# A hybrid decoder block on one core: first weight casts on VectorE, two early input tiles, norm 2's first product in token halves, residual products ahead at the end

## The chip, the cores and the metric

One NeuronCore of one Trainium2 chip runs the whole block in one launch. The metric is the device time of that core in microseconds, as the median of several runs; lower is better.

## The reference

One layer, T = 512 tokens of D = 1024 channels, all float32. The convolution branch has 1024 channels, the recurrence 1280, the channel mixer 2816.

```python
h = rmsnorm(x, norm1_g)
z = h @ w_in + b_in                      # 1024 -> 6656
z_glu, z_rx, z_rg, z_ga, z_gb = split(z) # 2048, 1280, 1280, 1024, 1024
u = z_glu[:, :1024] * sigmoid(z_glu[:, 1024:])
u = silu(layernorm(causal_depthwise_conv(u, 31 taps)))
y_a = u @ conv_w_out + conv_b_out
hb = rg_lru(causal_depthwise_conv(z_rx, 4 taps), wa, ba, wx, bx, lambda)
y_b = (hb * gelu(z_rg)) @ lru_w_out
x = x + (sigmoid(z_ga) * y_a + sigmoid(z_gb) * y_b) @ w_mix_out
h = rmsnorm(x, norm2_g)
x = x + (silu(h @ ffn_w1) * (h @ ffn_w3)) @ ffn_w2
return rmsnorm(x, norm_f_g)
```

## The kernel before

**Number format.** Every float32 operand of a matmul is split into a high part in float32r and a low part, the difference (`split_to`, L121: a cast by `copy`, ScalarE's unless told otherwise, then a subtraction on GpSimd or VectorE). One product of the reference is three on TensorE: high by high, high by low, low by high (`mm3`, L514). With `lo_last`, all products that need only the high weights come first.

**Weights.** They arrive in chunks of 128 x 1024 (`emit_chunk`, L145): a load by SyncE's queue into one of four buffers (`raws`, names raw_...), the cast on ScalarE, the difference on GpSimd (for w_in) or VectorE (later weights), into one of five split buffers (`hls`, names hl_...). `weights(key, ahead)` (L178) emits chunks up to four beyond the one wanted. Only chunks of w1 and w3 for norm 2 and what follows it are made from two loads; some of them are sums of four quarters that VectorE adds (L351) or a DMA accumulates (L349).

**Order.** A scheduler orders each engine's instructions by their dependences and by the order of the program. Inside `tc.manual_schedule(engines=...)` the listed engines keep the order in which the code is written; `tc.issue_after` puts work behind a named instruction. PSUM has six banks under `bank` and two under `bank2`.

**Start (L493 to L618).** TensorE first multiplies a tile of ones by itself (WARM times, one multiply is two records in the profile). The input comes in four row blocks of 128 tokens. `norm1_rows` (L575) takes a block's sum of squares and scales it in place (L579). Parameter vectors are loaded as rows (`load_rows`, L469) and transposed by TensorE (`rows_turned`, L503): norm1_g and b_in are the first group, since `turn_half` (L556) needs norm1_g. `turn_half` transposes 128 x 128 blocks of one half of the tokens (256), scales them by the norm's parameter on ScalarE (the high part, h, L566) and takes the low part on VectorE (L567). While the second half of the tokens is not there yet, the first EARLY_IN output tiles of w_in are computed on the first half alone (`early_mm`, L586): EARLY = 2 makes four tiles (0, 8, 1, 9), two of them started ahead of the second turn and two behind it; then all four are finished on the second half. The other tiles take all 512 columns in one matmul. PE, ScalarE, VectorE and SyncE are in written order here.

**Middle.** `ORDER` (L227) lists the tiles of w_in and the steps of the recurrence; the 31-tap convolution runs on VectorE beside it (`beside`, L670). `Quartered` and `Sevenfold` (L250, L896) form the products with w_mix_out and ffn_w2 from seven block products in place of eight.

**Norm 2 (L1006 to L1136).** `mix_end` ends the first residual sum, takes the norm's sums and transposes the first half of the tokens, in written order on PE, ScalarE and VectorE; its last lines emit one weight chunk and scale row blocks 2 and 3. The channel mixer's 22 output tiles of w1 and w3 go in pairs k and k + 11. Pairs 1 and 2 (FIRST) begin with two block products on the first token half (`f_product`, L1054, PSUM names fr1, fr2), which cover the wait for blocks 2 and 3. Then the second half is turned (L1076), with ScalarE's h and VectorE's low parts as at the start; VectorE also forms the plain sum of high and low, h2f (`full`, L1071), first for token half LO, and for HI within `f_inputs` (L1083), which makes the operands of the seven products from it. Pair 0 (PLAIN) is computed as plain products, first f1_0 and f3_0, then tiles 11. `ended` and `f_out` (L1111, L1115) finish the products of FIRST with a silu on ScalarE; then come the first products of pairs 3 and 4 (NEXT), and the others (PSUM names fa, fb, fe, ft).

**End (L1170 to L1225).** `out_end` adds up the second residual sum in four row blocks, two halves each. Blocks 0 and 1 are ready while TensorE still works (`finish(0)`, `finish(1)`); for blocks 2 and 3 the second half is ready early, the first half is in PSUM (r1) and gets its last products from `third` (hold = 3 of them kept back). `finish` (L1181) squares both halves with a sum on ScalarE, takes the reciprocal root, multiplies each half by the root and norm_f_g, and stores both. With `rest` (blocks 2 and 3), the product of the second half with norm_f_g is taken ahead of `third` and scaled by ScalarE behind it:

```python
begun = rstd_begin(x2[t][1], jk[0])
if rest:
    vec.tensor_tensor(out=o[1], in0=x2[t][1], in1=gf[1], op=ALU.mult)
    rest()
r = rstd_end(begun, first, jk[1])
```

Of the kernel before, what the change touches and what calls it, by code (L numbers as in the profile page):

```python
# [13 lines left out]
P = 128  # L14
# [11 lines left out]
NT = T // P  # L26
# [10 lines left out]
WARM = 12  # L37
# [49 lines left out]
def tile_block(ctx, tc, a, out):  # L87
# [33 lines left out]
    def split_to(h, l, full, eng, copy=act.copy):  # L121
# [9 lines left out]
        return h, l  # L131

    def split(name, full, eng, p_=None, copy=act.copy):
        p_ = p_ or pairt(name)
        return split_to(*p_, full, eng, copy)
# [9 lines left out]
    def emit_chunk():  # L145
# [16 lines left out]
        if where != "long":  # L162
            hl = hls.tile([P, 2, 1024], F32R, tag="hl", name=f"hl_{key}")
            h, l = split_to(hl[:, 0, :n], hl[:, 1, :n], rv, lo)
# [9 lines left out]
    def emit_to(n):  # L174
        while emitted[0] < min(len(chunks), n):
            emit_chunk()
# [278 lines left out]
    row_at = lambda c: (0, c) if c < n_first else (1 + (c - n_first) // P, (c - n_first) % P)  # L455
# [44 lines left out]
    for i in first:  # L500
        load_rows(i)
# [54 lines left out]
    def turn_half(name, rows, gname, dest, hf, bk, some=range(ND)):  # L556

        cs = slice(hf * 256, hf * 256 + 256)
        for c in some:
# [5 lines left out]
            h, l = (v[:, cs] for v in dest[c])  # L565
            act.activation(h, ps[:, :256], AF.Copy, scale=g)  # L566
# [15 lines left out]
    EARLY = 2  # L582
# [12 lines left out]
    with tc.manual_schedule(engines={ET.PE, ET.Activation, ET.DVE, ET.SP}):  # L595
        norm1_rows(0)
        norm1_rows(1)
        rows_turned(0, n_first)
        emit_to(1)
        turn_half("tx", xt, "norm1_g", h1p, 0, [bank, bank, bank, bank2])  # L600
        emit_to(2)
        load_x(2)
        load_x(3)
        norm1_rows(2)
        norm1_rows(3)
        emit_to(3)
# [7 lines left out]
        early_mm(2, 0)  # L614
        early_mm(3, 0)
        rows_turned(n_first, n_rows)
        for i in range(4):
            early_mm(i, 1)  # L618
# [457 lines left out]
    turned = turn_half("th", xs, "norm2_g", h2p, 1, [bank2])  # L1076
    h2 = parts_of(h2p)
    with tc.issue_after(turned):
        emit_to(emitted[0] + 3)
# [3 lines left out]
    def f_inputs(ks):  # L1083
        for k in ks:
            a1, a2 = h2f[k], h2f[k + 4]
            full(k, HI)
            full(k + 4, HI)
# [23 lines left out]
    def ended(k, c11, r2):  # L1111
        add(c11, r2, c11)
        f_out(c11, o7.uv[k][0][:, LO])
# [8 lines left out]
    for i, j in enumerate((PLAIN, PLAIN + KF)):  # L1122
        p1, p3 = bank(f"f1_{j}"), bank(f"f3_{j}")
        mm3(p1, w_tiles(f"f1_{j}", ND), h2)
        mm3(p3, w_tiles(f"f3_{j}", ND), h2)
# [55 lines left out]
    def finish(t, ps=None, rest=None):  # L1181
# [3 lines left out]
        first = x2[t][0] if ps is None else ps  # L1185
        begun = rstd_begin(x2[t][1], jk[0])
        if rest:
            vec.tensor_tensor(out=o[1], in0=x2[t][1], in1=gf[1], op=ALU.mult)
            rest()
        r = rstd_end(begun, first, jk[1])  # L1190
        vec.scalar_tensor_tensor(out=o[0], in0=first, scalar=r, in1=gf[0], op0=ALU.mult, op1=ALU.mult)
        if rest:
            act.activation(o[1], o[1], AF.Copy, scale=r)
        else:
            vec.scalar_tensor_tensor(out=o[1], in0=x2[t][1], scalar=r, in1=gf[1], op0=ALU.mult, op1=ALU.mult)
# [3 lines left out]
    def out_end(second, plus, r1, r2, r7, third):  # L1199
# [18 lines left out]
        finish(0)  # L1218
        for k in range(kh - hold, kh):
            outq.get(k, "t4")  # L1220
        finish(1)
        for i in range(2):
            finish(2 + i, r1[i], lambda: third(i, range(kh - hold, kh)))
# [35 lines left out]
```

## Time and profile before

| | |
|---|---|
| device time, median of 3 runs | 800.8 us (800.53 to 800.96) |
| profiled execution: its own time | 800.93 us |
| profiled execution: span | 799.2 us, mean granted TensorE clock 0.998 |
| TensorE matmul (PE) | 788.9 us, 99% of the span |
| TensorE weight load (PEld) | 689.5 us, 86% |
| VectorE (DVE) | 675.5 us, 85% |
| ScalarE (ACT) | 472.1 us, 59% |
| GpSimd (POOL) | 231.6 us, 29% |
| DMA | 140.29 MB, mean 176 GB/s |

In rows of the profile, PE is the matmul side of TensorE, PEld its weight load, DVE VectorE, ACT ScalarE, POOL GpSimd, and SPq SyncE's queue. A row of the order of time has the start in us from the start of the span, the time taken in us, the engine, the line of the kernel (L123), the operation, what it writes <- what it reads, shapes, and a count where equal neighbours are joined; in square brackets stands what the engine waited for and how long. A row of groups has the count, then least, median and greatest duration in ns, then the time from the first to the last. In the waits, "PE tx L563 <- DVE x L579: 0.9, 2, 0.6" reads: TensorE's instructions of L563 that write tx waited for VectorE's L579 0.9 us in total, two times, 0.6 at the longest. The time of one matmul record covers a pipelined operation, so its pace is read from start to start.

### The profile page before, as it was taken

How to read it: one execution, taken by the hardware profiler on the slowest of the kernel's cores; microseconds unless marked ns; L12 is line 12 of the kernel's file. 1: busy time of each engine (PE TensorE's matmuls, PEld its weight loads, DVE VectorE, ACT ScalarE, POOL GpSimd, SP SyncE). 2: the span in 40 equal slices, each digit the busy share in tenths (PEclk: the TensorE clock that was granted, in tenths of full speed). 3: DMA queues.
4: the chain of work that ended last, by engine and by line, in shares of the span. 5: the costliest groups of instructions: out<-in, count | busy, mean ns of one | idle time of the engine just before them, and what ended most of it. 6: DMA issues, size and time to landing. Idle time of an engine off the chain costs nothing.

```text
span 799.2 us, 12191 instructions
## 1 busy us (share of the span) xinstructions
PE 788.9 (99%) x4374; PEld 689.5 (86%) x4374; DVE 675.5 (85%) x1027; ACT 472.1 (59%) x678; POOL 231.6 (29%) x182
## 2 busy tenths in 40 slices
PE   8999999999999999999999999999999999999997
PEld 7988888888888888888888888999999999888885
DVE  4699899999989988796787889978778887889756
ACT  7546595898668855563335574545455555577443
POOL 3565867687766855130000000000000000000000
PEclk9999999999999999999999999999999999999999
DMA  7945647378564754468947536477555553676552
GB/s 212 239 122 165 174 150 212 121 213 237 164 193 144 225 177 125 128 193 266 282 153 246 172 107 183 120 178 190 147 132 133 133 132 106 205 265 203 198 172 105
DMA packets 184624, 140.29 MB, mean 176 GB/s; under 512 B 14279, under 2 KB 162163, under 8 KB 184563
## 3 DMA queue, kind: packets, MB, share of 16 engines
q1 hardware_dynamic: 183123, 134.27, 55.4%
q0 software_dynamic: 1440, 5.24, 3.5%
q8 instruction: 34, 0.56, 0.3%
q14 instruction: 27, 0.22, 0.1%
HBM read 113.79 MB, written 18.64 MB: 166 GB/s over the span
## 4 chain that ended last, share of the span: by engine, by line
PE 91%; DVE 4%; DMA 2%; ACT 2%; issue 1%; SPq 0%; DVEq 0%; POOLq 0%; ACTq 0%
PE z L523 35%; PE or L933 13%; PE ft L1060 7%; PE yb L523 7%; PE fa L1060 6%; PE ya L523 5%; PE mxr L933 5%; PE fe L1060 3%; PE g L807 3%; PE fr L1060 3%; PE fb L1060 2%; PE f L523 1%; DMA raw_fb<-in_ffn_w_dram 1%; DMA raw_fb<-raw_fb 1%; DMA x<-in_x_dram 1%
## 5 line engine op out<-in xcount | busy, mean ns | idle before, releaser
L682 DVE SCALAR_TENSOR_TENSOR cv<-u,par,cv 128x511 f32<-128x511 f32 (+16 forms) x240 | 162.0, 728 | 2.3 <-ACT cv L679 2.2
L119 POOL TENSOR_TENSOR hl_in<-raw_in,hl_in 128x1024 fp32r<-128x1024 f32 x52 | 125.9, 2426 | 82.8 <-ACT hl_in L123 80.4
L349 POOL DMA_DIRECT2D raw_fb<-raw_fb x10 | 8.7, 874 | 299.3 <-DVE raw_fb L351 186.6
L119 POOL TENSOR_TENSOR ows<-ows 128x256 f32<-128x256 f32 x66 | 57.2, 870 | 37.5 <-DMA ows<-in_ffn_w_dram 34.5
L123 ACT CAST hl_in<-raw_in 128x1024 fp32r<-128x1024 f32 x52 | 54.2, 1043 | 10.2 <-PE z L523 6.5
L123 ACT CAST hl_ft<-raw_fb 128x1024 fp32r<-128x1024 f32 x40 | 41.8, 1048 | 28.9 <-DVE raw_fb L351 12.7
L119 DVE TENSOR_TENSOR hl_ft<-raw_fb,hl_ft 128x1024 fp32r<-128x1024 f32 x40 | 48.6, 1219 | 9.7 <-ACT hl_ft L123 9.6
L119 DVE TENSOR_TENSOR hl_fb<-raw_fb,hl_fb 128x1024 fp32r<-128x1024 f32 x30 | 36.6, 1220 | 9.2 <-ACT hl_fb L123 8.9
L523 PE MATMUL z<-h10h,hl_in 128*128 128x512 f32 (+1 forms) x112 | 42.2, 378 | 1.0 <-DVE h10l L567 1.0
L523 PE MATMUL z<-h13h,hl_in 128*128 128x512 f32 (+1 forms) x112 | 41.7, 374 | 0.0
L523 PE MATMUL z<-h14h,hl_in 128*128 128x512 f32 (+1 forms) x112 | 41.7, 374 | 0.0
L523 PE MATMUL z<-h15h,hl_in 128*128 128x512 f32 (+1 forms) x112 | 41.7, 374 | 0.0
L523 PE MATMUL z<-h11h,hl_in 128*128 128x512 f32 (+1 forms) x112 | 41.7, 374 | 0.0
L523 PE MATMUL z<-h16h,hl_in 128*128 128x512 f32 (+1 forms) x112 | 41.7, 374 | 0.0
L523 PE MATMUL z<-h17h,hl_in 128*128 128x512 f32 (+1 forms) x112 | 41.7, 374 | 0.0
L523 PE MATMUL z<-h12h,hl_in 128*128 128x512 f32 (+1 forms) x112 | 41.7, 374 | 0.0
L351 DVE TENSOR_TENSOR raw_fb<-raw_fb,raw_fb 128x1024 f32<-128x1024 f32 x20 | 24.5, 1225 | 16.9 <-DMA raw_fb<-in_ffn_w_dram 16.6
L119 DVE TENSOR_TENSOR hl_ob<-raw_ob,hl_ob 128x1024 fp32r<-128x1024 f32 (+1 forms) x23 | 27.0, 1172 | 10.5 <-ACT hl_ob L123 7.6
L123 ACT CAST hl_ob<-raw_ob 128x1024 fp32r<-128x1024 f32 (+1 forms) x23 | 23.4, 1016 | 20.7 <-PE or L933 14.7
L123 ACT CAST hl_fb<-raw_fb 128x1024 fp32r<-128x1024 f32 x30 | 31.4, 1047 | 6.7 <-PE mxr L933 3.7
L1060 PE MATMUL fe<-hs_0h,hl_ft 128*128 128x256 f32 x160 | 30.8, 284 | 0.4 <-DVE hl_ft L119 0.4
L1060 PE MATMUL ft<-hs_1h,hl_ft 128*128 128x256 f32 x160 | 30.4, 283 | 0.0
(965 smaller groups left out, 2610.1 us busy)
## 6 DMA issues: line engine op xcount, KB each, us to landing
raw_in<-in_w_in_dram SPq DMA_DIRECT2D x52, 512.0 KB
raw_fb<-in_ffn_w_dram SPq DMA_DIRECT2D x96, 256.0 KB
ows<-in_ffn_w_dram SPq DMA_DIRECT2D x44, 256.0 KB
os<-ows SPq DMA_DIRECT2D x22, 512.0 KB
raw_ob<-in_ffn_w_dram SPq DMA_DIRECT2D x33, 256.0 KB
raw_ot<-os SPq DMA_DIRECT2D x33, 256.0 KB
raw_lo<-in_lru_w_out_dram SPq DMA_DIRECT2D x16, 320.0 KB
raw_fb<-raw_fb POOLq DMA_DIRECT2D x10, 512.0 KB, 4.5
```

Of the source, the lines that this page charges most:

```text
L119: return eng.tensor_tensor(out=o, in0=x, in1=y, op=ALU.subtract)
L123: copy(h, full)
L349: pool_e.dma_start(out=q, in_=y, accum_op=ALU.add)
L351: vec.tensor_tensor(out=q, in0=q, in1=y, op=ALU.add)
L523: pe.matmul(ps, l, r, start=i == 0, stop=i == n - 1)
L682: vec.scalar_tensor_tensor(out=acc[c][:, s:], in0=u[c][:, : T - s], scalar=dw(c, s), in1=acc[c][:, s:], op0=ALU.mult, op1=ALU.add)
L807: pe.matmul(ps, l, r, start=k == 0, stop=k == len(mms) - 1)
L933: pe.matmul(banks[i], l_[:, ts], r_, start=start and n == 0, stop=stop and n == 2, skip_group_check=again)
L1060: pe.matmul(ps[:, HALVES[i]], lw[:, 4 * i + c, :], rx_, start=not (again or i or c or m), stop=bool(i and c == 3 and m == 2), skip_group_c ...
```

## The change

- WARM goes from 12 to 21.
- The casts of the first two weight chunks are done by VectorE (`vec.tensor_copy`), no longer by ScalarE. The third chunk is emitted behind the loads of all parameter rows, with the fourth.
- EARLY goes from 2 to 1: two tiles of w_in (0 and 8) are worked in token halves. Both start on the first half ahead of the second turn; both are finished behind it. The transposes of b_in's rows move behind the second turn, into a tile of their own; b_in's rows are loaded behind x's blocks 2 and 3.
- Norm 2: TensorE's order from the second turn on is written by hand. f1_0 is computed in token halves in four steps, each of four transposes (two channel blocks of the second half) and twelve matmuls of 256 columns. For this half, ScalarE writes h2f itself from the transposes (`full` given), casts the high part from it, and VectorE takes the difference; `f_inputs` no longer adds up h2f for HI. f3_0 takes the low weights last. The silu of FIRST comes behind the last h2f.
- End: `finish` is split. The squares and products of the second halves of blocks 2 and 3 are written ahead of both `third`. Blocks 0 to 2 get their second half by that product and a scaling on VectorE; only block 3 is scaled by ScalarE.

```diff
@@ -34,7 +34,7 @@
 RAW = 4
 HL = 5
 AHEAD = 4
-WARM = 12
+WARM = 21
 
 FEW, MANY = 32, 112
 
@@ -128,11 +128,11 @@
             last = sub(eng, l, full, h.bitcast(F32))
         if eng is pool_e:
             newest["sub"] = last.ins
-        return h, l
+        return h, l, last
 
     def split(name, full, eng, p_=None, copy=act.copy):
         p_ = p_ or pairt(name)
-        return split_to(*p_, full, eng, copy)
+        return split_to(*p_, full, eng, copy)[:2]
 
 
     chunks = []
@@ -142,7 +142,7 @@
     def wchunk(key, src, kt, cols, where="hl", lo=pool_e, after=None):
         chunks.append((key, src, kt, cols, where, lo, after))
 
-    def emit_chunk():
+    def emit_chunk(copy=act.copy):
         if emitted[0] == GATES_AT:
             load_gates()
         key, src, kt, cols, where, lo, after = chunks[emitted[0]]
@@ -161,7 +161,7 @@
             newest["load"] = nc.sync.dma_start(rv.rearrange("p (k n) -> p k n", k=kt), src).ins
         if where != "long":
             hl = hls.tile([P, 2, 1024], F32R, tag="hl", name=f"hl_{key}")
-            h, l = split_to(hl[:, 0, :n], hl[:, 1, :n], rv, lo)
+            h, l, _ = split_to(hl[:, 0, :n], hl[:, 1, :n], rv, lo, copy)
             if after:
                 after(rv, h)
             held[key] = (h.rearrange("p (k n) -> p k n", k=kt), l.rearrange("p (k n) -> p k n", k=kt))
@@ -171,9 +171,9 @@
                 for i in range(2)
             ]
 
-    def emit_to(n):
+    def emit_to(n, copy=act.copy):
         while emitted[0] < min(len(chunks), n):
-            emit_chunk()
+            emit_chunk(copy)
 
     def weights(key, ahead=AHEAD):
         i = next(i for i, c in enumerate(chunks) if c[0] == key)
@@ -452,7 +452,12 @@
     n_rows = sum(n for _, n in ROWS)
     n_first = ROWS[0][1] + ROWS[1][1]
     par = consts.tile([P, n_rows], F32, name="par")
-    row_at = lambda c: (0, c) if c < n_first else (1 + (c - n_first) // P, (c - n_first) % P)
+    starts = (0, ROWS[0][1], n_first)
+
+    def row_at(c):
+        b = sum(c >= s_ for s_ in starts) - 1
+        return b + (c - starts[b]) // P, (c - starts[b]) % P
+
     at, col, parts = 0, {}, []
     for name, n in ROWS:
         col[name] = at
@@ -497,8 +502,7 @@
     first = [i for i, (lo, _, _) in enumerate(parts) if lo < n_first]
     load_x(0)
     load_x(1)
-    for i in first:
-        load_rows(i)
+    load_rows(first[0])
 
     def rows_turned(c0, c1):
         pt = bank2(f"par_ps{c0}")
@@ -553,7 +557,7 @@
             between()
         return rstd_end(begun, halves[1], junk[1])
 
-    def turn_half(name, rows, gname, dest, hf, bk, some=range(ND)):
+    def turn_half(name, rows, gname, dest, hf, bk, some=range(ND), full=None):
 
         cs = slice(hf * 256, hf * 256 + 256)
         for c in some:
@@ -563,6 +567,11 @@
                 pe.transpose(ps[:, t * P : (t + 1) * P], src, ident)
             g = pc(gname, c)
             h, l = (v[:, cs] for v in dest[c])
+            if full:
+                f = full[c][:, cs]
+                newest["half"] = act.activation(f, ps[:, :256], AF.Copy, scale=g).ins
+                _, _, last = split_to(h, l, f, vec)
+                continue
             act.activation(h, ps[:, :256], AF.Copy, scale=g)
             last = vec.scalar_tensor_tensor(out=l, in0=ps[:, :256], scalar=g, in1=h.bitcast(F32), op0=ALU.mult, op1=ALU.subtract)
         return last.ins
@@ -579,7 +588,7 @@
             vec.tensor_scalar(out=xt[t][h], in0=xt[t][h], scalar1=r, scalar2=None, op0=ALU.mult)
 
     HALVES = [slice(0, 256), slice(256, 512)]
-    EARLY = 2
+    EARLY = 1
     EARLY_IN = [(GLU + j + 8 * o) for j in range(EARLY) for o in range(2)]
     early = []
 
@@ -595,15 +604,16 @@
     with tc.manual_schedule(engines={ET.PE, ET.Activation, ET.DVE, ET.SP}):
         norm1_rows(0)
         norm1_rows(1)
-        rows_turned(0, n_first)
-        emit_to(1)
+        rows_turned(0, ROWS[0][1])
+        emit_to(1, vec.tensor_copy)
         turn_half("tx", xt, "norm1_g", h1p, 0, [bank, bank, bank, bank2])
-        emit_to(2)
+        emit_to(2, vec.tensor_copy)
         load_x(2)
         load_x(3)
+        for i in first[1:]:
+            load_rows(i)
         norm1_rows(2)
         norm1_rows(3)
-        emit_to(3)
         for i in range(len(parts)):
             if i not in first:
                 load_rows(i)
@@ -611,11 +621,10 @@
         early_mm(1, 0)
         turn_half("tx", xt, "norm1_g", h1p, 1, [bank2, bank, bank])
         emit_to(4)
-        early_mm(2, 0)
-        early_mm(3, 0)
+        for i in range(2):
+            early_mm(i, 1)
+        rows_turned(ROWS[0][1], n_first)
         rows_turned(n_first, n_rows)
-        for i in range(4):
-            early_mm(i, 1)
     h1 = parts_of(h1p)
 
 
@@ -1073,8 +1082,17 @@
 
     for c in range(ND):
         full(c, LO)
-    turned = turn_half("th", xs, "norm2_g", h2p, 1, [bank2])
     h2 = parts_of(h2p)
+    plain_1 = bank(f"f1_{PLAIN}")
+    with tc.manual_schedule(engines={ET.PE}):
+        ws = w_tiles(f"f1_{PLAIN}", ND, 0)
+        for q in range(4):
+            cs, ks = HALVES[q // 2], range(4 * (q % 2), 4 * (q % 2) + 4)
+            turned = turn_half("th", xs, "norm2_g", h2p, 1, [bank2], range(2 * q, 2 * q + 2), h2f)
+            for k in ks:
+                (wh, wl), (xh, xl) = ws[k], (v[:, cs] for v in h2[k])
+                for m, (l, r) in enumerate(((wh, xh), (wh, xl), (wl, xh))):
+                    pe.matmul(plain_1[:, cs], l, r, start=k == 0 and m == 0, stop=k == ND - 1 and m == 2)
     with tc.issue_after(turned):
         emit_to(emitted[0] + 3)
 
@@ -1083,8 +1101,6 @@
     def f_inputs(ks):
         for k in ks:
             a1, a2 = h2f[k], h2f[k + 4]
-            full(k, HI)
-            full(k + 4, HI)
             g = [longt(f"hs{k}_{i}") for i in range(2)]
             s1, s2, s3, s4 = (v[:, cs] for v in g for cs in HALVES)
             sub(vec, s1, a2[:, HI], a1[:, HI])
@@ -1110,7 +1126,8 @@
 
     def ended(k, c11, r2):
         add(c11, r2, c11)
-        f_out(c11, o7.uv[k][0][:, LO])
+        with tc.issue_after(newest["half"]):
+            f_out(c11, o7.uv[k][0][:, LO])
 
     def f_out(c, dst, sign=1.0):
         s_ = shortt("sl")
@@ -1120,9 +1137,10 @@
     for k in FIRST:
         ended(k, begun(k, first[k][0]), first[k][1])
     for i, j in enumerate((PLAIN, PLAIN + KF)):
-        p1, p3 = bank(f"f1_{j}"), bank(f"f3_{j}")
-        mm3(p1, w_tiles(f"f1_{j}", ND), h2)
-        mm3(p3, w_tiles(f"f3_{j}", ND), h2)
+        p1, p3 = bank(f"f1_{j}") if i else plain_1, bank(f"f3_{j}")
+        if i:
+            mm3(p1, w_tiles(f"f1_{j}", ND), h2)
+        mm3(p3, w_tiles(f"f3_{j}", ND), h2, lo_last=not i)
         ffn_out(j, p1, p3)
         if i == 0:
             f_inputs(range(2, 4))
@@ -1178,21 +1196,22 @@
         for h in range(2):
             nc.sync.dma_start(gf[h], a["norm_f_g"][h * T : (h + 1) * T].partition_broadcast(P))
 
-    def finish(t, ps=None, rest=None):
+    def finish_begin(t):
 
         o = [longt(f"of{t}{i}") for i in range(2)]
         jk = [bank(f"jk{t}{i}") for i in range(2)]
-        first = x2[t][0] if ps is None else ps
         begun = rstd_begin(x2[t][1], jk[0])
-        if rest:
-            vec.tensor_tensor(out=o[1], in0=x2[t][1], in1=gf[1], op=ALU.mult)
-            rest()
-        r = rstd_end(begun, first, jk[1])
+        vec.tensor_tensor(out=o[1], in0=x2[t][1], in1=gf[1], op=ALU.mult)
+        return o, jk[1], begun
+
+    def finish(t, o, jk, begun, first):
+
+        r = rstd_end(begun, first, jk)
         vec.scalar_tensor_tensor(out=o[0], in0=first, scalar=r, in1=gf[0], op0=ALU.mult, op1=ALU.mult)
-        if rest:
+        if t == NT - 1:
             act.activation(o[1], o[1], AF.Copy, scale=r)
         else:
-            vec.scalar_tensor_tensor(out=o[1], in0=x2[t][1], scalar=r, in1=gf[1], op0=ALU.mult, op1=ALU.mult)
+            vec.tensor_scalar(out=o[1], in0=o[1], scalar1=r, scalar2=None, op0=ALU.mult)
         for i in (0, 1):
             nc.sync.dma_start(o_nat[:, t, i * T : (i + 1) * T], o[i])
 
@@ -1215,12 +1234,14 @@
                     seed = add(r1[i], r1[i], x2[2 + i][0])
                     if i == 0:
                         newest["tie"] = seed.ins
-        finish(0)
+        finish(0, *finish_begin(0), x2[0][0])
         for k in range(kh - hold, kh):
             outq.get(k, "t4")
-        finish(1)
+        finish(1, *finish_begin(1), x2[1][0])
+        begun = [finish_begin(2 + i) for i in range(2)]
         for i in range(2):
-            finish(2 + i, r1[i], lambda: third(i, range(kh - hold, kh)))
+            third(i, range(kh - hold, kh))
+            finish(2 + i, *begun[i], r1[i])
 
     o7.run(x2, loads, out_end)
```

## The prediction

> **What bounds the kernel now.** I read the page first (shares, chain), then the waits of TensorE, then the order of time in the three stretches that the edits touch.
>
> ```profile
> span 799.2 us, 12191 instructions
> PE 788.9 (99%) x4374; PEld 689.5 (86%) x4374; DVE 675.5 (85%) x1027; ACT 472.1 (59%) x678; POOL 231.6 (29%) x182
> PE 91%; DVE 4%; DMA 2%; ACT 2%; issue 1%; SPq 0%; DVEq 0%; POOLq 0%; ACTq 0%
> PE tx L563 <- DVE x L579: 0.9, 2, 0.6
> PE fe L1060 <- DVE hl_ft L119: 0.4, 1, 0.4
> PE f L523 <- ACT h20h L566: 0.4, 1, 0.4
> ```
>
> TensorE is busy for 99% of the span and carries 91% of the chain that ended last. So a microsecond is won only if TensorE has less to do, or stands less in the places that the waits view lists (us in total, times, longest): the turn of the input (tx) and norm 2 with what follows it (f, fe). A tail after its last matmul comes on top. All three edits lie there. A faster VectorE or ScalarE elsewhere brings nothing.
>
> Two paces price TensorE's work:
>
> ```profile
> 24.54 0.28 PE L523 MATMUL z<-h14h,hl_in 128*128 128x256 f32 x1
> 24.66 0.28 PE L523 MATMUL z<-h14l,hl_in 128*128 128x256 f32 x1
> 485.17 0.39 PE L523 MATMUL f<-h25l,hl_f 128*128 128x512 f32 x1
> 485.40 0.39 PE L523 MATMUL f<-h25h,hl_f 128*128 128x512 f32 x1
> ```
>
> From start to start, 256 columns take 0.12 us and 512 take 0.227 (24 of them 5.44). A product of 24 matmuls done in two token halves therefore costs 48 x 0.12 - 5.44 = 0.32 us more than done whole.
>
> **Part 1, the start.**
>
> ```profile
> 1.08 5.49 PE L495 MATMUL warm<-ones 128*128 128x128 f32 x24 [1.08 <-DVE ones L488]
> 8.18 1.86 PE L563 MATMUL tx<-ident,x 128*128 128x128 f32 x15 [0.64 <-DVE x L579]
> 9.09 1.05 ACT L123 CAST hl_in<-raw_in 128x1024 fp32r<-128x1024 f32 x1 [1.69 <-DMA raw_in<-in_w_in_dram]
> 10.54 0.48 DVE L567 SCALAR_TENSOR_TENSOR h10l<-tx,par,h10h 128x256 fp32r<-128x256 f32 x1 [1.90 <-ACT h10h L566]
> 13.29 0.47 DVE L567 SCALAR_TENSOR_TENSOR h17l<-tx,par,h17h 128x256 fp32r<-128x256 f32 x1
> 12.91 1.09 ACT L123 CAST hl_in<-raw_in 128x1024 fp32r<-128x1024 f32 x1
> 14.08 2.41 POOL L119 TENSOR_TENSOR hl_in<-raw_in,hl_in 128x1024 fp32r<-128x1024 f32 x1 [1.48 <-ACT hl_in L123]
> 15.79 1.38 DVE L579 TENSOR_SCALAR x<-x,stats 128x512 f32<-128x512 f32 x2
> 18.40 2.24 PE L563 MATMUL tx<-ident,x 128*128 128x128 f32 x15 [0.26 <-DVE x L579]
> L579 DVE TENSOR_SCALAR x<-x,stats x8: 473/484/983, 5.4 to 18.3; 128x512 f32<-128x512 f32 x8
> L219 DVE CAST hl_gate<-raw_gate x6: 283/283/805, 54.8 to 227.0; 32x256 fp32r<-32x256 f32 x6
> 500.92 1.22 DVE L351 TENSOR_TENSOR raw_fb<-raw_fb,raw_fb 128x1024 f32<-128x1024 f32 x1
> ```
>
> Two input tiles fewer are split into halves: 2 x 0.32 = 0.64 us less for TensorE, certain. One more small transpose of parameter rows (0.12, by 1.86/15) takes some back: +0.5.
>
> The rest hangs on when the second half can be turned, 18.40 before. There the chain runs: second cast (ends 14.0), GpSimd's difference (14.08 to 16.49), and x scaled only as GpSimd ends: one of the eight scalings took 983 ns, not 484, and it is in the pair at 15.79. From GpSimd's end to the turn are 1.9 us. If GpSimd did not hold the scaling up, it could begin once the second cast and two small instructions are through, 14.6 by my estimate (14.05 below, and 0.5) in place of 15.79, and the turn would come 1.2 us earlier; I do not count on it, because of the 983 ns. The Trainium skill, page "SBUF — State Buffer", section "Who interferes with whom", has VectorE's two-port copies and GpSimd lock one another out of a shared port pair for a whole instruction. By that rule the scaling waits here too, and the 1.2 us are not to be had; the trace agrees.
>
> The casts now stand in VectorE's queue, and ScalarE's eight h no longer wait behind the one of 9.09. What a 1024-column cast costs VectorE no row shows. Below: 0.48 (a 512-column scaling); above: 1.22 (a 1024-column sum, the last row). The steps 283 ns for 256 and 484 for 512 continue to 0.9, which I take. Added warm-up: 12 multiplies took 5.49 us, so nine more cost up to 4.1 us at 0.457 each, and 1.1 at a transpose's 0.124; they start at 6.6 and the turn stood at 8.18, so they delay it by 0 to 2.5 us. The transposes at 8.18 run at about their pace in norm 2 (below), so TensorE is no longer slow by then: I take 0.4. The Trainium skill, page "TensorE: Matmul & The Clock Gate", Part 1, would have the clock double after some 3.4 us of work; by that the nine take about 2.05 us and end at 8.6, an estimate that gives the same 0.4.
>
> Then, the cast beginning as before when its load is in, 9.1: cast to 10.0; eight low halves at (13.29 - 10.54)/7 = 0.39 until 13.15; second cast to 14.05. Before it was 14.0, so the turn stays at 18.4. Casts at 0.48 bring it 0.8 us forward, casts at 1.22 put it back by 0.7; warm-ups at the slow pace end at 10.7, 2.1 later, of which 0.5 hides behind the load: 1.6 more. Part 1 is +0.5 us, between -1.8 and +1.3.
>
> SyncE's queue: the 52 rows of b_in pass behind x, and the third weight load goes from 8.7 behind the parameter rows.
>
> ```profile
> 17.52 2.69 SPq L161 DMA_DIRECT2D raw_in<-in_w_in_dram x3
> 21.95 1.05 ACT L123 CAST hl_in<-raw_in 128x1024 fp32r<-128x1024 f32 x1 [0.16 <-DMA raw_in<-in_w_in_dram]
> ```
>
> It then stands where the load issued at 17.52 stood, is cast at 21.95 and has its low half at 21.95 + 1.05 + 2.4 = 25.4. TensorE wants it at 18.4 + 2.24 + 5.76 = 26.4: hidden, with 1 us to spare; past that each microsecond late costs one.
>
> **Part 2, norm 2.**
>
> ```profile
> 456.06 1.03 PE L563 MATMUL th<-ident,xs 128*128 128x128 f32 x8
> 456.85 0.48 PE L933 MATMUL mxr<-mxt42h,mxvb2h 128*128 128x512 f32 x1
> 464.76 1.22 DVE L119 TENSOR_TENSOR hl_fb<-raw_fb,hl_fb 128x1024 fp32r<-128x1024 f32 x1
> 469.84 1.05 ACT L123 CAST hl_f<-raw_f 128x1024 fp32r<-128x1024 f32 x1 [0.52 <-DMA raw_f<-in_ffn_w_dram]
> 472.07 0.60 PE L563 MATMUL th<-ident,xs 128*128 128x128 f32 x4
> 472.52 0.46 ACT L566 ACTIVATE h20h<-th,par 128x256 fp32r<-128x256 f32 x1
> 472.61 3.30 DMA raw_fb<-in_ffn_w_dram
> 475.99 1.05 ACT L123 CAST hl_fb<-raw_fb 128x1024 fp32r<-128x1024 f32 x1 [0.51 <-DMA raw_fb<-in_ffn_w_dram]
> 486.39 0.62 ACT L123 CAST hs_0h<-hs 128x512 fp32r<-128x512 f32 x1 [3.11 <-DVE hs L1093]
> 496.96 0.28 PE L1060 MATMUL fr<-h20h,hl_fb 128*128 128x256 f32 x1
> 515.04 0.50 PE L1060 MATMUL fe<-hs_0h,hl_ft 128*128 128x256 f32 x2 [0.41 <-DVE hl_ft L119]
> ```
>
> From 472.07 to 496.96, 24.9 us, TensorE does 16 transposes and 96 matmuls. The matmuls are 96 x 0.227 = 21.8, the transposes 16 x 0.10 = 1.6 (eight between 456.06 and 456.85). So 1.5 us are waits, small ones around each turn, since ScalarE interleaves table load, copies and casts with the eight h. The change works the first product in halves (+0.32) and lays its ready low half beside the turn: each quarter is four transposes and twelve matmuls, 0.4 + 1.44 = 1.84 us. ScalarE's four instructions in a quarter are two activations of 0.46 and two 256-column casts (between half of the 512-column one, 0.31, and all of it, 0.62; I take 0.35, since most of the 0.62 goes by columns: the 1024-column cast takes 1.05): 1.6. VectorE's two differences are 0.8 at the pace of the low halves. TensorE paces; 1.5 - 0.3 - 0.1 for turning between shapes = +1.1.
>
> Cover: in the new order ScalarE casts the next weights (b11 of column 3) right ahead of the first turned tile. That cast waits for its load and for the last product before the turn: 472.1 to 473.1. TensorE has done its first twelve matmuls at 472.07 + 1.84 = 473.9 and then needs two tiles read, 473.1 + 2 x 0.46 = 474.0: no slack is left. The load is issued once VectorE is through two differences of 1.22 that begin at 464.76, so at 467.2; at 3.3 us from issue to landing it is in by 470.5.
>
> The delayed silus of the first columns wait for the turn; behind them on ScalarE stand the cast of the following weights and the silu of the first product, none wanted by TensorE before 496. VectorE loses eight additions of 256 columns (about 3 us at 0.39 each) between turn and fe.
>
> ```profile
> 502.72 4.65 DMA raw_fb<-raw_fb
> ```
>
> The wait of 0.41 us at 515.04 is the end of a chain from the sum at 500.92 (last row of part 1's fence) over the accumulating DMA. That sum stands behind VectorE's work after the last f product; with this 1.1 us earlier and less in its queue, it comes some 1.6 us earlier, and the wait goes: +0.4 (at worst 0). Part 2 is +1.5 us, between -0.5 (ScalarE's casts at 0.62: four quarters of 2.2 against 1.84, and the late start) and +1.9.
>
> **Part 3, the end.**
>
> ```profile
> 792.85 0.39 PE L933 MATMUL or<-hl_ot,ovb10l 128*128 128x512 f32 x1
> 792.95 0.72 ACT L1193 ACTIVATE of<-of,stats 128x512 f32<-128x512 f32 x1 [0.23 <-DVE stats L547]
> 793.58 0.58 ACT L545 ACTIVATE jk<-or 128x512 f32<-128x512 f32 x1
> 794.83 0.75 DVE L1191 SCALAR_TENSOR_TENSOR of<-or,stats,gfh 128x512 f32<-128x512 f32 x1
> ```
>
> The last matmul ends at 793.24, but the last square begins at 793.58, behind ScalarE's scaling for the third row block. The change gives that scaling to VectorE (0.48, in the gap before 794.8) and squares the residual halves ahead. The square begins at 793.28: +0.3. What is late next is the same path, square to store, unchanged. VectorE's added products lie before TensorE's end; were they late, 0.
>
> **Sum.** 0.5 + 1.5 + 0.3 = 2.3 us. The profiled execution took 800.93 us with its span of 799.2; the median is 800.8. From either, 2.3 less is 798.6 and 798.5; I say 798.5.
>
> **Rivals.** (a) TensorE's place is taken by the helpers: VectorE's casts and the warm-ups turn the second half later (part 1 at -0.7 or so), or ScalarE paces norm 2 (part 2 at +0.3). For it: no slack at the first tile, and casts whose price no row shows. Against: 1.6 a quarter against 1.84. It gives 0.5 to 1.4 us less than before, 799.4 to 800.3.
>
> (b) Slower: the cast of the next weights holds up ScalarE's queue, and with it the whole turn. Before, this load landed at 475.9. Each microsecond that it lands after 472.1 is one for TensorE, which has the turn's order fixed. Landing at 475.9 costs 3.8: 800.8 - 2.3 + 3.8 = 802.3; landing at 477, 803.4. From 474.4 on it decides against the change. For it: the load ahead of it on the queue was itself waited for, at 469.84. Against: it is now issued some 5 us earlier.
>
> (c) GpSimd's difference does not hold up the second half's scaling, and the turn comes 1.2 us earlier: 797.3. Against it: the 983 ns.
>
> **How the numbers follow.** Forecast 0.58 (797.7 to 799.2); (a) 0.24; (b) 0.08; (c) 0.10. The range of 8 in 10 reaches over (a) and most of (c): 797.3 to 800.4. 0.2%, 1.6 us, is about what a measurement of this kernel can tell from no change. Faster by more: forecast, (c) and a little of (a), 0.72. Within: the rest of (a) and a third of (b), 0.21. Slower: the rest of (b) and what I overlook, 0.07.
>
> **What would show it.** Part 1: second turn at 18.4 and the first 512-column z about 0.5 us earlier against it; wrong if the turn moves past 19 or the third tile waits for its load. Part 2: the stretch from turn to the NEXT products 23.8 us and no wait at fe; wrong if a tile's transposes wait for ScalarE behind a cast of hl_fb. Part 3: last square 0.04 us after the last matmul. The forecast is wrong if any of these parts comes out negative, or if a wait appears between 40 and 450 us, where I move nothing.

## The result, and the profile after

The changed kernel takes 808.01 us (median of 5 runs, 805.44 to 808.07) against 800.96 us before (800.53 to 801.42, 5 runs): ratio 1.0074, interval 1.0063 to 1.0085. The forecast was 798.5, between 797.3 and 800.4. Its profiled execution took 805.44 us with a span of 803.7; that is the shortest of the five (see e12).

The page of the changed kernel, then the waits of TensorE (us in total, times, longest):

```profile
PE 790.8 (98%) x4369; PEld 690.8 (86%) x4369; DVE 684.6 (85%) x1025; ACT 472.3 (59%) x684; POOL 230.4 (29%) x182
PE 86%; DVE 10%; ACT 1%; DMA 1%; issue 0%; POOL 0%; SPq 0%; POOLq 0%; ACTq 0%
```

```profile
PE z L527 <- DVE xb L828: 5.1, 1, 5.1
...
PE tx L567 <- DVE x L588: 0.5, 1, 0.5
PE g L816 <- ACT ext L791: 0.5, 1, 0.5
```

The waits of f and fe are gone, as meant, and with them one of z for h10l (1.0 us at the start). In their place stands one wait of 5.1 us in a stretch that the change does not touch: a tile of w_in needs a PSUM bank that VectorE's recurrence step L828 (L819 before) still reads. VectorE's share of the chain that ended last went from 4% to 10%. First that step and the tile behind it before, then TensorE's order of time around the wait after, with the step in its last line, and the granted clock there (windows: us, PE busy, PEclk, DMA share, GB/s):

```profile
107.18 0.68 DVE L819 SCALAR_TENSOR_TENSOR xb<-g,xb 128x512 f32<-128x512 f32 x1
110.22 0.39 PE L523 MATMUL z<-h10h,hl_in 128*128 128x512 f32 x1
```

```profile
109.00 0.39 PE L527 MATMUL z<-h17h,hl_in 128*128 128x512 f32 x1
114.53 0.79 PE L527 MATMUL z<-h10h,hl_in 128*128 128x512 f32 x1 [5.14 <-DVE xb L828]
115.12 0.63 PE L527 MATMUL z<-h10l,hl_in 128*128 128x512 f32 x1
115.54 0.63 PE L527 MATMUL z<-h10h,hl_in 128*128 128x512 f32 x1
...
113.79 0.68 DVE L828 SCALAR_TENSOR_TENSOR xb<-g,xb 128x512 f32<-128x512 f32 x1
```

```profile
114.00:116.00 2.00, 1.47 (x4) 0.63 0.53 141
116.00:118.00 2.00, 2.00 (x6) 0.52 0.69 201
```

Before, the step ended 2.4 us ahead of the tile (107.86 and 110.22); after, it ends 6.6 us later. The wait also costs the clock. Behind it 512 columns take 0.43 us from start to start in place of 0.227 until about 118: 1.5 us more. The Trainium skill, page "TensorE: Matmul & The Clock Gate", Part 1, says that an idle window of some 3.4 us takes the clock down by half and that the window runs freely; from 100 us on the runs below agree: waits of 3.8 us and more are followed by a granted clock of 0.5, waits up to 2.3 us are not. At the start, shorter ones can be followed by it too (see e5).

Why is VectorE late? Its order of time before, from the parameter arithmetic (softplus of lru_lambda, 10 columns an instruction) to the convolution (cv) and the second channel (u, its second row), and GpSimd's differences in the same stretch:

```profile
31.16 2.42 DVE L637 TENSOR_TENSOR sm<-sm 128x10 f32<-128x10 f32 x1
34.64 2.35 DVE L639 TENSOR_TENSOR sm<-sm 128x10 f32<-128x10 f32 x1
39.29 3.12 DVE L682 SCALAR_TENSOR_TENSOR cv<-u,par,cv 128x511 f32<-128x511 f32 x4 [0.85 <-ACT cv L679]
42.32 0.74 DVE L746 SCALAR_TENSOR_TENSOR u<-z,par,sg 128x512 f32<-128x512 f32 x1
...
31.15 2.40 POOL L119 TENSOR_TENSOR hl_in<-raw_in,hl_in 128x1024 fp32r<-128x1024 f32 x1 [3.31 <-ACT hl_in L123]
34.56 2.40 POOL L119 TENSOR_TENSOR hl_in<-raw_in,hl_in 128x1024 fp32r<-128x1024 f32 x1 [1.01 <-ACT hl_in L123]
```

The same of the changed kernel:

```profile
28.96 0.95 DVE L639 TENSOR_SCALAR sm<-sm 128x10 f32<-128x10 f32 x1 [1.25 <-ACT sm L638]
30.19 2.19 DVE L641 TENSOR_TENSOR sm<-sm 128x10 f32<-128x10 f32 x1
32.41 2.31 DVE L642 TENSOR_TENSOR sm<-sm 128x10 f32<-128x10 f32 x1
34.76 2.33 DVE L644 TENSOR_SCALAR sm<-sm 128x10 f32<-128x10 f32 x1
37.71 2.33 DVE L646 TENSOR_TENSOR sm<-sm 128x10 f32<-128x10 f32 x1
40.07 2.32 DVE L647 TENSOR_SCALAR sm<-sm 128x10 f32<-128x10 f32 x1
42.42 0.17 DVE L646 TENSOR_TENSOR sm<-sm 128x10 f32<-128x10 f32 x1
44.77 0.75 DVE L691 SCALAR_TENSOR_TENSOR cv<-u,par,cv 128x511 f32<-128x511 f32 x1
50.15 0.74 DVE L755 SCALAR_TENSOR_TENSOR u<-z,par,sg 128x512 f32<-128x512 f32 x1
...
27.48 9.59 POOL L119 TENSOR_TENSOR hl_in<-raw_in,hl_in 128x1024 fp32r<-128x1024 f32 x4 [3.36 <-ACT hl_in L123]
37.61 4.75 POOL L119 TENSOR_TENSOR hl_in<-raw_in,hl_in 128x1024 fp32r<-128x1024 f32 x2
```

An instruction of 0.17 us takes 2.2 to 2.4 where a difference of GpSimd runs beside it (0.95 where it begins midway): it ends only when the difference does. Before, two met one; GpSimd stood idle between. After, six differences stand close behind one another from 27.48 to 42.36, and six instructions are shut out, 11.4 us beyond their own time in place of 4.4. So the second channel starts 7.8 us later (50.15 for 42.32). VectorE cannot make that up. In the windows view of before it is busy 211.85 of the 220 us from 40 to 260:

```profile
40.00:260.00 220.00, 220.00 (x970) 181.85 (x970) 211.85 (x323) 157.57 (x200) 154.23 (x121) 1.00 0.59 173
```

(us, then busy time of PE, PEld, DVE, ACT, POOL.) The stations of TensorE, from both orders of time:

| from, to | before, us | after, us |
|---|---|---|
| span's start to first product of gate 1 | 83.84 | 82.84 |
| to first transpose of norm 2 | 372.22 | 379.23 |
| to second turn (th) | 16.01 | 16.02 |
| to first product of NEXT | 24.89 | 24.05 |
| to end of the last matmul | 296.28 | 295.90 |
| to the end of the span | 5.96 | 5.66 |

All the loss is in the second row: 7.0 us, of which 5.1 are the wait and 1.5 the clock; 0.4 I can't assign. The other rows gain 2.5, so this execution is 4.5 us longer than the profiled one of before; the medians lie 7.05 apart, for which see e12.

### The profile page after: what moved, and what is told of

It reads as the page before. It is cut to its first block, busy times and chain, and to the rows that moved or that the text cites. A ratio compares the mean times of both kernels' runs of the same rounds, so it can differ in the third digit from the quotient of the medians.

```text
span 803.7 us, 12183 instructions
## 1 busy us (share of the span) xinstructions
PE 790.8 (98%) x4369; PEld 690.8 (86%) x4369; DVE 684.6 (85%) x1025; ACT 472.3 (59%) x684; POOL 230.4 (29%) x182
## 4 chain that ended last, share of the span: by engine, by line
PE 86%; DVE 10%; ACT 1%; DMA 1%; issue 0%; POOL 0%; SPq 0%; POOLq 0%; ACTq 0%
PE z L527 25%; PE or L942 13%; PE ft L1069 7%; PE yb L527 7%; PE fa L1069 6%; PE fr L1069 6%; PE ya L527 5%; PE mxr L942 5%; DVE cv L691 5%; PE fe L1069 4%; PE fb L1069 2%; PE f L527 2%; PE g L816 2%; DVE xb L769 1%; PE f L1095 1%
## 5 line engine op out<-in xcount | busy, mean ns | idle before, releaser
L691 DVE SCALAR_TENSOR_TENSOR cv<-u,par,cv 128x511 f32<-128x511 f32 (+17 forms) x240 | 162.5, 729 | 1.1 <-ACT cv L688 0.8
L123 ACT CAST hl_in<-raw_in 128x1024 fp32r<-128x1024 f32 x50 | 51.8, 1043 | 6.9 <-PE z L527 3.6
```

What stands on the lines that cost most here:

```text
L123: copy(h, full)
L691: vec.scalar_tensor_tensor(out=acc[c][:, s:], in0=u[c][:, : T - s], scalar=dw(c, s), in1=acc[c][:, s:], op0=ALU.mult, op1=ALU.add)
```

## The experiments

Theory: the new start lays GpSimd's differences over VectorE's parameter arithmetic, and VectorE, nearly full until 260 us, carries that lateness to L828. Rivals: the tiles 1 and 9 come later on TensorE and that alone makes the convolution late; or the loss sits in norm 2 or at the end. "Shut out" counts parameter instructions of over 0.9 us; u1 is the start of the second channel; the ratio is to the runs of before on the same chip.

| run | shut out | u1, us | wait for L828, us | median, us | ratio (95%) |
|---|---|---|---|---|---|
| before | 2 | 42.32 | 0 | 800.96 | |
| after | 6 | 50.15 | 5.14 | 808.01 | 1.0074 (1.0063, 1.0085) |
| e1 start undone | 2 | 42.29 | 0 | 799.69 | 0.9977 (0.9969, 0.9986) |
| e2 start alone | 6 | 50.51 | 5.30 | 809.73 | 1.0104 (1.0088, 1.0120) |
| e3 arithmetic in PSUM | 0 | 39.29 | 0 | 800.41 | 0.9982 (0.9973, 0.9990) |
| e4 series cut short | 5 | 46.13 | 1.02 | 801.89 | 1.0008 (0.9998, 1.0017) |
| e5 EARLY 2, rows last | 3 | 48.58 | 0 | 807.99 | 1.0075 (1.0062, 1.0088) |
| e6 third load ahead | 5 | 49.72 | 3.81 | 806.55 | 1.0056 (1.0042, 1.0071) |
| e7 casts on ScalarE | 6 | 50.66 | 5.30 | 807.33 | 1.0063 (1.0049, 1.0077) |
| e8 before, longer series | 3 | 47.01 | 1.00 | 804.37 | 1.0031 (1.0020, 1.0043) |
| e9 EARLY 2, rows as before | 2 | 45.19 | 0 | 803.30 | 1.0022 (1.0013, 1.0031) |
| e10 rows between | 4 | 46.97 | 0.77 | 810.40 | 1.0112 (1.0098, 1.0126) |
| e11 rows between, PSUM | 0 | 40.32 | 0 | 808.15 | 1.0081 (1.0068, 1.0095) |
| e12 changed kernel again | 6 | 50.94 | 5.15 | 807.30 | 1.0070 (1.0057, 1.0083) |
| e13 EARLY 1 alone | 5 | 48.90 | 3.93 | 804.70 | 1.0038 (1.0024, 1.0051) |
| e14 casts on VectorE alone | 2 | 41.49 | 0 | 798.84 | 0.9966 (0.9954, 0.9979) |
| e15 e14 and PSUM | 0 | 41.25 | 0 | 799.86 | 0.9981 (0.9972, 0.9991) |
| e16 e13 and PSUM | 0 | 40.48 | 0 | 799.95 | 0.9976 (0.9968, 0.9985) |

**e1, e2: where the loss is.** e1 takes the start of before into the changed kernel, e2 the changed start into the kernel before.

```diff
-    EARLY = 1
+    EARLY = 2
...  (e1: with it WARM, the casts, the order of loads and row transposes)
```

> Changed kernel with the start as before (WARM 12, casts on ScalarE, four early tiles, row loads as before); norm 2 and end as changed. Lock theory (the loss comes from VectorE's small parameter instructions, L635 to L653, shut out by GpSimd's differences, which the new start puts back to back): no long wait of z, 799.4 us = 800.96 - 0.8 (norm 2) - 0.4 (fe) - 0.3 (end). Rival (the loss sits in norm 2 or at the end, and the wait at 109 us only shifts it): above 803.

> Kernel before with the changed start alone. Lock theory: the whole loss is here, 808.0 + 1.5 = 809.5 us, a wait of z for L828 of 5 us or more and half clock behind it. Rival: about 800.

Both as the theory has it. The start carries all of the loss, and norm 2 and the end together gain 0.23% (0.14 to 0.31), near 1.8 us.

**e3, e4: is it the shutting out?** e3 lays the intermediate values on a PSUM tile, so that no instruction has two inputs in SBUF, and none with a single input has both input and output there (one product is written twice for it); e4 leaves out the later terms of the series.

```diff
-    ab, e, s, s2, po, c4 = (sm[:, i, :] for i in range(6))
+    ab, s, s2, cm, c4 = (sm[:, i, :] for i in range(5))
+    smp = bank("smp")
+    e, t_, po, c4p = (smp[:, 16 * i : 16 * i + NR] for i in range(4))
```

> Changed kernel, the small parameter instructions on a PSUM tile (one operand of each there) so that they need not share GpSimd's way to SBUF. Lock theory: none takes over 0.5 us, the first step of the convolution is at about 39 us and not 44.8, the wait of z is gone, 798.4 us. Rival (with two early tiles the second channel's tiles, 1 and 9, come later on TensorE, and that makes the convolution late; the locked instructions are incidental): 805 to 808, the wait stays near 5 us.

> Changed kernel with n_terms 2 in place of 9: 14 of the small instructions are left out, so the series of softplus is cut short. Lock theory: four of the six locked instructions go, some 9 us of VectorE, the wait of z goes: 798.4 to 800. Rival (late tiles 1 and 9): 805 to 808.

VectorE's and GpSimd's order of time in e3:

```profile
29.57 0.18 DVE L641 TENSOR_SCALAR smp<-smp 128x10 f32<-128x10 f32 x1 [1.24 <-ACT smp L640]
33.12 0.76 DVE L694 SCALAR_TENSOR_TENSOR cv<-u,par,cv 128x511 f32<-128x511 f32 x1 [0.19 <-ACT cv L691]
39.29 0.75 DVE L758 SCALAR_TENSOR_TENSOR u<-z,par,sg 128x512 f32<-128x512 f32 x1 [0.55 <-ACT sg L756]
...
28.12 9.59 POOL L119 TENSOR_TENSOR hl_in<-raw_in,hl_in 128x1024 fp32r<-128x1024 f32 x4 [3.38 <-ACT hl_in L123]
```

GpSimd's run of differences is the same as after; no instruction waits for it any more, u1 starts at 39.29, and the wait is gone. That decides for the theory: the tiles 1 and 9 stand where they stood. The Trainium skill, page "SBUF — State Buffer", section "Who interferes with whom", has it so: instructions with two SBUF inputs, or in a two-port mode, are shut out by GpSimd for its whole instruction, those with at most one SBUF input, outside such a mode, are not. e3 was 1 us slower than I expected against its own chip's runs of before; TensorE waits 1.13 us for an ext tile at 159, which is of that size, but no run tests it. e4 fell short (801.89 for 798.4 to 800): I had taken four of the six to be in the loop that it shortens, but only two were; four are among those it keeps, a fifth (L653) is shut out besides, and the wait shrank to 1.02 and did not go.

**e8: lateness alone.** The kernel before with nothing but more of the small instructions.

```diff
-    n_terms = 9
+    n_terms = 18
```

> Kernel before, nothing of the change, with n_terms 18: 18 more of the small instructions (3.7 us at 0.205 from start to start, and 2.2 for each one that GpSimd shuts out), so VectorE reaches the convolution 4 to 10 us later. Lock theory: lateness of VectorE alone is enough; its slack is some 2.4 us (L828's forerunner ends at 107.9 where z is wanted near 110.2), so TensorE waits for L819 2 to 7 us and the time is 803 to 809. Rival (the order of tiles or the free PSUM banks of the new start make the wait): 801, no wait.

u1 at 47.01 and a wait of 1.00 for L819: lateness of VectorE is enough to make it. It was shorter than the expected 2 to 7, since only three instructions were shut out; the profiled execution is 3.9 us longer than that of before (the medians on its chip lie 2.6 apart), and of the other 2.9 us it shows small waits (0.7 at a turn of norm 2, 0.8 at fe) and a start 0.3 later. Over all runs but e5 and e9, where TensorE itself is 3 to 4 us late by gate 0, the wait grows nearly as fast as u1 moves: 0.8 to 1.0 at 46 to 47, 3.8 to 3.9 at 49 to 50, 5.1 to 5.3 at 50 to 51. By that pace it begins once u1 starts past some 45 us, an estimate.

**e5, e6, e7, e9: which part of the start?** Each puts one part back: EARLY 2 (e5, e9 with the row transposes ahead of the second halves again), the third weight load ahead of the rows (e6), the casts on ScalarE (e7).

```diff
         norm1_rows(3)
+        emit_to(3)          # e6
...
-        emit_to(1, vec.tensor_copy)
+        emit_to(1)          # e7, and emit_to(2)
```

> Changed kernel with EARLY 2 again (four tiles in token halves), all else of the changed start kept. Lock theory with two early tiles as its cause (tile pair 0 done at 25 us frees weight buffers and a silu of its own at once, so that GpSimd's differences run back to back from 27 to 42 us): the run of differences has gaps again, two locked instructions at most, no wait of z; 799 to 800.5 us. If the later row and weight loads are the cause: 805 to 808.

> Changed kernel with the third weight chunk emitted ahead of the parameter rows, as before. If the load behind the rows is what bunches the differences: at most three locked instructions, the wait below 1 us, 799 to 801. If two early tiles are the cause: five or six locked instructions still, 804 to 808.

> Changed kernel with the first two casts on ScalarE again. Both variants of the lock theory: the differences still run back to back, the wait stays near 5 us, 806 to 809, with the second turn about 0.5 to 1 us later than with casts on VectorE. If the casts on VectorE are what makes VectorE late: 799 to 801.

> Changed kernel with EARLY 2 and, as before, the transposes of the parameter rows ahead of the four second halves (e5 had them behind all four, at 41.7 us). Lock theory with two early tiles as the cause of the run of differences: at most three locked instructions, u1 by 45 us, no wait of z, 799 to 800.5. If another part of the start is the cause: u1 near 50 us and 805 to 808.

e6 and e7 clear the load order and the casts: the differences still stand close, and the wait is 3.8 and 5.3. e5 was not a clean test. With four tiles ahead of the row transposes the parameters arrive at 41.7 us, and VectorE is late for that reason: TensorE has small waits of 0.2 to 1.3 in five places behind 160 us. It also waits 2.13 us at 22.47 for a cast of tile 1, and the clock halves behind that until 26.9; e9 has the same wait and keeps its clock, so at the start the length of one wait does not decide. The windows from 24 to 26 of e5, then of e9:

```profile
24.00:26.00 2.00, 2.00 (x11) 0.50 1.22 290
24.00:26.00 2.00, 1.70 (x14) 1.00 1.22 286
```

e9 puts the row transposes back ahead of the second halves. Two instructions are shut out and no tile waits for L828, so EARLY 1 (with the row transposes where it puts them) is what makes the run of differences. e9 still misses its 799 to 800.5: with the third load behind the rows, tile 1 waits 2.13 us for its cast, which four early tiles lay open.

**e13, e16: EARLY 1 alone, with and without the shutting out.** The start as before but for EARLY 1; the later row transposes stand behind its two second halves.

> Start as before (WARM 12, casts on ScalarE, loads as before), norm 2 and end changed, and EARLY 1 as the only part of the new start, with the transposes of the later parameter rows behind the two second halves. If the two early tiles make the run of differences: five or six locked instructions, u1 near 50 us, wait of z 3.5 to 5.5, half clock behind it, 804 to 808. If it takes the other parts of the start too: as e1, 799 to 801.

> As e13, with the small instructions on a PSUM tile. Lock theory: the wait of z of e13 goes with the locks, 798.5 to 800.5. If it is the later tiles 1 and 9: as e13.

```profile
112.79 0.50 PE L523 MATMUL z<-h10h,hl_in 128*128 128x512 f32 x1 [3.93 <-DVE xb L822]
```

This row of e13 has no counterpart in e16, where no tile waits for that line; both came out as expected. 4.75 us of medians lie between the two, from the place of ten-column operands (and one product written twice) alone. Before, the longest of GpSimd's gaps in this stretch (3.31 us, ahead of 31.15) came with a cast that waited for a split buffer which the four early tiles still held. It stands in ScalarE's order of time of before:

```profile
30.03 1.05 ACT L123 CAST hl_in<-raw_in 128x1024 fp32r<-128x1024 f32 x1 [1.62 <-PE z L523]
```

The next gap (1.01 us) came with a table load and a sigmoid ahead of the cast on ScalarE, not with a buffer. In the changed kernel two early tiles give their buffers back by 25.2 us, and no weight cast ahead of 220 us waits for TensorE. That last link is read from the traces, not tested by itself.

**e10, e11: the parameters earlier.** The row transposes between the two second halves.

```diff
-        for i in range(2):
-            early_mm(i, 1)
+        early_mm(0, 1)
         rows_turned(ROWS[0][1], n_first)
         rows_turned(n_first, n_rows)
+        early_mm(1, 1)
```

> Changed kernel with two early tiles, the parameter rows transposed between the second halves of tiles 0 and 8, some 3 us earlier, so that the small instructions begin at about 23 us, where GpSimd is idle for some 3.4 us, and not at 26.6. Lock theory: two to four of them locked in place of six, u1 by 42 to 47 us, wait of z 0 to 1.5 us, 799 to 802.5. Rival (lateness comes with the tiles 1 and 9): 805 to 808.

> The last one with the small instructions on a PSUM tile as in e3. Lock theory: none locked, u1 by 39 us, no wait of z; 798.5 to 800.5. If VectorE's whole queue up to 260 us is the bound behind it, no better than e3 (0.9982 of before).

Wrong: 7.9 and 7.7 us above the upper ends of the ranges, for another cause. In e10 the shutting out, u1 and the wait for L828 came out as expected. e11 shuts nothing out, has u1 at 40.32 and no wait for L828, and yet:

```profile
183.45 0.38 SPq L161 DMA_DIRECT2D raw_in<-in_w_in_dram  x1
183.94 0.54 SPq L799 DMA_DIRECT2D ext6h<-xb7h  x1
...
180.48 0.68 DVE L119 TENSOR_TENSOR xb7l<-xb,xb7h 128x512 fp32r<-128x512 f32 x1
...
188.78 0.76 PE L819 MATMUL g<-ext6h,hl_gate 112*128 112x512 f32 x1 [4.99 <-DMA ext6h<-xb7h]
```

These are SyncE's queue, VectorE and TensorE of e11. The gate's matmul waits 4.99 us for the copy of ext6h, and the clock halves again (0.50 from 188 to 194); e10 waits 5.17 there. The copy stands in SyncE's queue behind a weight load and is issued 2.8 us after VectorE is through with xb7. In e3 that distance is nearly the same, 2.5 us, but all of it lies 6.2 to 6.5 us earlier:

```profile
173.88 1.08 DVE L119 TENSOR_TENSOR xb7l<-xb,xb7h 128x512 fp32r<-128x512 f32 x1
...
177.41 1.22 SPq L799 DMA_DIRECT2D ext6h<-xb7h  x1
```

So it is VectorE that is late. Between the product of u (166.40 in e3, 167.88 in e11) and xb7l it does two steps of the convolution in e3 and ten in e11, some 5 us more. Why the scheduler orders them otherwise was not taken apart.

**e12: the spread of the changed kernel.**

> The changed kernel once more, for a profile of one of its usual executions (807.4 to 808.1; the profiled one took 805.4). Lock theory: beside the wait of z for L828 of about 5 us stands a second, shorter wait between 120 and 280 us for VectorE's late recurrence (L830, or ext6h copied from it), 1 to 2.5 us. Rival: the start itself took longer in those, the first turn 2 us later.

Its profiled execution took 807.72 us. The wait is the same (5.15); a second one of 0.21 stands at 190, so the theory's second wait is not the reason. The second turn starts at 18.09 in place of 17.32, and the clock stays low longer:

```profile
114.00:118.00 4.00, 2.68 (x6) 0.50 0.76 205
118.00:120.00 2.00, 2.00 (x6) 0.50 0.30 79
120.00:122.00 2.00, 2.00 (x9) 0.90 0.28 75
```

Half clock holds until about 120.2, not 118, which costs some 2.3 us in place of 1.5. With 0.8 at the start that is 1.6 of the 2.3 us between the two executions.

**e14, e15: what is worth keeping.** The start as before with only the first two casts on VectorE; e15 with the arithmetic in PSUM.

```diff
-        emit_to(1)
+        emit_to(1, vec.tensor_copy)
...
-        emit_to(2)
+        emit_to(2, vec.tensor_copy)
```

> Start as before with only the first two casts on VectorE; norm 2 and end changed. Lock theory: two locked instructions as before, no wait of z, and the second turn up to 1 us earlier: 798.5 to 799.7, against 0.9977 of before for e1. If casts on VectorE put it behind: above 800.5.

> As e14, with the small instructions on a PSUM tile. Lock theory: none locked, the convolution begins some 4 us earlier, but TensorE waited for nothing there, so the time is that of e14 within 0.5 us.

e14 is the fastest of all, 0.34% below before (0.21 to 0.46); its lead on e1 lies within the intervals. e15 does not gain on it, since nothing waits for the convolution there. It misses both its expectations: the medians lie 1.0 us apart, not 0.5, and the second channel begins 0.2 us earlier, not 4, since the parameters come 2.3 us later. It loses 0.7 and 0.3 us in early tiles whose casts wait for their loads (1.53 and 0.74 us; in e14 0.17 and 1.15); whether that belongs to the execution or to the edit is not shown.

## Why the prediction was wrong

**The step that failed** is the bound that it drew at the start: "A faster VectorE or ScalarE elsewhere brings nothing", and part 1 priced only what stands on TensorE's way to the second turn. A slower VectorE was not asked about. Part 1 moved work of GpSimd and of VectorE against each other between 27 and 42 us, and the prediction followed neither past the turn. It had the row that warns of it (983 ns for a scaling beside GpSimd, and the rule on it), used it for one instruction, and did not look for others: the 2.42 of L637 stands in the trace of before. What the runs show in its place: VectorE had 2.4 us of slack at L819, the new start made L828 6.6 us later, and TensorE paid 5.1 us of wait and 1.5 of clock. Its own condition named the outcome, "if a wait appears between 40 and 450 us, where I move nothing". Nothing was moved there in the code; its start was.

No rival had this. (b), the slower one, put the loss in norm 2, where the cast of the next weights did not hold ScalarE up.

**Part 1 by its terms.** These rows of the changed kernel answer it:

```profile
8.41 0.68 DVE L123 CAST hl_in<-raw_in 128x1024 fp32r<-128x1024 f32 x1
12.25 0.68 DVE L123 CAST hl_in<-raw_in 128x1024 fp32r<-128x1024 f32 x1
13.61 2.48 DVE L588 TENSOR_SCALAR x<-x,stats 128x512 f32<-128x512 f32 x2
13.01 2.40 POOL L119 TENSOR_TENSOR hl_in<-raw_in,hl_in 128x1024 fp32r<-128x1024 f32 x1 [1.44 <-DVE stats L544]
17.32 2.24 PE L567 MATMUL tx<-ident,x 128*128 128x128 f32 x15 [0.52 <-DVE x L588]
```

The cast takes 0.68 (I took 0.9, between 0.48 and 1.22) and begins at 8.41, not 9.1, so the second one ends at 12.93, not 14.05, and GpSimd's difference and the turn move up with it: the turn came at 17.32, 1.1 earlier. The scaling is shut out again, its pair 2.48 long while GpSimd works until 15.4, so (c) did not come, though by the earlier casts the turn came nearly as early as (c) has it. The added warm-ups took 1.46 us and put off nothing (first turn 8.12 for 8.18; I took 0.4). From the second turn to gate 0 TensorE took 52.06 against 52.69 (the wait of 0.46 not counted in either): the 0.63 of two whole tiles, as worked out. The third load was hidden. On TensorE's way part 1 gained 1.7 us by gate 0 (71.09 to 69.38), above its +1.3; 0.7 of it were lost again by gate 1, and what it started elsewhere cost 7.0. Some of the gain belongs to this execution: e12, the same kernel, has its turn at 18.09 and reaches gate 0 at 70.16, gate 1 at 83.62. Even with nothing shut out the new start is no faster than the old (e3 0.9982 of before, e1 0.9977).

**Part 2** held: 24.05 us from turn to NEXT for 23.8 forecast, quarters of 1.86 to 1.90 for 1.84, no wait at fe:

```profile
478.09 0.60 PE L567 MATMUL th<-ident,xs 128*128 128x128 f32 x4
479.95 0.63 PE L567 MATMUL th<-ident,xs 128*128 128x128 f32 x4
502.14 0.28 PE L1069 MATMUL fr<-h20h,hl_fb 128*128 128x256 f32 x1
```

It gains 0.84 there and 0.38 behind, 1.2 for 1.5; e1 has 0.86 and 0.37. The size depends on the execution of the old norm 2 that it is held against: e2 and e8, which keep it, take 25.39 and 25.41 there and 0.9 to 1.1 more behind than before did, with 0.8 to 1.2 us of waits at fe.

**Part 3** held to a tenth:

```profile
797.65 0.39 PE L942 MATMUL or<-hl_ot,ovb10l 128*128 128x512 f32 x1
798.08 0.58 ACT L549 ACTIVATE jk<-or 128x512 f32<-128x512 f32 x1 [1.02 <-PE or L942]
```

The last square starts 0.04 us after the last matmul (798.04) as forecast, and the tail is 5.66 us in place of 5.96.

## What to carry to other kernels

An engine that is off the chain but nearly full in a stage is a bound with a little slack: price what an edit does to the moment at which it enters that stage, not only what it does to the engine that bounds. When an edit changes when weight buffers come free, list what runs on the two engines that share a way to memory in the microseconds behind it; six tiny instructions cost VectorE 11.4 us here, and the kernel more than the matmuls that were saved. Moving their values to another memory took that cost away without a change in their order.

## What was not expected of the hardware

An instruction over 10 columns with two SBUF inputs, or a tensor_scalar from SBUF to SBUF, stretches from 0.17 to 2.2 to 2.4 us beside a GpSimd difference of 2.4, scalar_tensor_tensor too (2.31 in e1); the same with one of them in PSUM keeps its 0.17 to 0.18. A TensorE wait of 3.8 to 5.3 us from 100 us on is followed by half clock until 3.5 to 5.8 us behind its end, which adds 1.5 us in the profiled execution of the changed kernel and 2.3 in e12; waits of 1.0 to 2.3 us there are not. In the first 30 us a wait of 2.13 us was followed by half clock in e5 and not in e9.
